# A new order of loads at the pass boundaries, and a new end, in an encoder layer with Strassen-Winograd products

## The chip, the cores and the metric

The kernel runs on one core of one Trainium2 chip. The metric is the device time of one execution in microseconds (us). Timed three times, the kernel before took 2190.53, 2190.92 and 2191.3 us; the median is 2190.92 us.

## The reference

One layer of a streaming encoder, on 2048 prompt rows and 32 rows of a later chunk, with the same weights:

```
h = rms_norm(x, g_mix); p = h @ w_in
mix = concat(pool, conformer conv, short conv, chunk gMLP)(p)
x = x + mix @ w_out
f = rms_norm(x, g_ffn)
x = x + (silu(f @ w_gate) * (f @ w_up)) @ w_down
y = rms_norm(x, g_final)
```

The model width is 1024, the width of w_gate and w_up is 2816. All inputs and outputs are float32. Beside y, the last input rows of the mixers are returned as their new states; the change doesn't touch them.

## The kernel before

**Arithmetic.** Every matrix product is made in three passes of TensorE: an operand is split into a high part (a cast by ScalarE) and a low part (the operand minus its high part), and high x high, low x high and high x low are added up in PSUM. So each weight tile costs a load, a ScalarE cast and a GpSimd subtraction before TensorE can use it, and each row tile costs a cast and a subtraction that GpSimd and VectorE share.

**Stages.** Rows lie as columns (model width on the partitions). The mixer part works in 5 chunks of 416 columns and ends with `w_out_pass(2)`, which finishes `x2[3]` and `x2[4]`. The FFN part works in 6 chunks of 348 or 346 columns, two in each of three passes (`FPASSES`). In a pass the loop over `g` (11 times, `NG`) makes a pair of hidden blocks: `ffn_pair` (L1212) runs `block` once for w_gate (`gate`) and once for w_up (`up`). A block is one Strassen-Winograd product: seven forms named p1, p5, p7, p6, p2, p3, p4 (`ORDER`), each of 12 matmuls (`wide`). After each form stands `then` (L1182), and `step[0]` counts the forms.

**Weights.** `operands` (L1023) loads the four quarters a11, a21, a22, a12 of a block's weights (256 KB each, tag raw, 5 buffers) and makes the seven left operands from them, four of them by additions on VectorE (L1048 to L1059, tile `sum`); `weight_parts` splits each (L1019 on ScalarE, L1020 on GpSimd). `Ahead` makes them `LEAD` = 4 steps before they are used, and loads a block's quarters two at a time.

**Down products.** While a pair is computed, the product of the pair before with w_down is worked off, one `down` (6 matmuls into a `pd` bank of PSUM, then the VectorE addition `xs<-pd,xs` at L1153) after each form or a little oftener, from `LAG` = 3 steps after its pair. 16 of them belong to a pair (8 row tiles m, 2 chunks). Their weights come in four quarters by `quarters` (L1236): two loads of 128 KB (tag rawd, 4 buffers), cast `dhi` (L1253), subtraction `dlo` (L1254).

**Right operands of a pass.** `sums_of` and `first_operands` write the seven row operands to DRAM (`td`). `part` (L953) brings one in, in three steps: the DMA, the cast on ScalarE (L960), the subtraction, half on GpSimd and half on VectorE (L963). They lie in a pool of 5 large tiles (`bigp`), which in the mixers hold `x2[0]` to `x2[4]`. `next_part` (L1431) issues the DMA at one step, and the cast and the subtraction together two steps later.

**Turn of a pass.** When the last pair's down products of a half (m = 3, m = 7) are done, `turn_over` (L1396) writes the two chunks' finished half to DRAM (`away`) and loads the next pass's residual into the same tile (`residual`, `xs<-x2d`). Then `finish` reads the rows back, forms the final norm and writes y.

**The first pair.** Its raw weights go into two tiles that the mixers no longer need (a11, a21, a22, a12 in halves), and a12 and a22 are loaded a second time into `late` tiles (L1056).

**The end.** The last pair's 16 down products run chunk after chunk. For the first chunk of the two, `finish_here` (generator) is worked on between the products of the second, for which squares are made by ScalarE (L1500), added in twos by GpSimd (L1502), and summed over the partitions by small matmuls (L1298) after m = 1, 3, 5, 6 and 7. Then come reciprocal root (L1294), diagonal (L1410), spread over the partitions by a matmul (L1513), scaling of 8 row tiles and the store.

**What sets the order.** Each engine works strictly in the order in which its instructions are issued, the DMA queue of SyncE (SP) too: a DMA that must wait holds all behind it. VectorE and TensorE follow the program text throughout; ScalarE, GpSimd and SP do from the FFN part on. Generators in a list (`ahead`) are advanced by `fill` after each form.

Of the kernel before, what the change touches and what calls it, by code (L numbers as in the profile page):

```python
# [85 lines left out]
def trunk_kernel(ctx: ExitStack, tc: tile.TileContext, a):  # L86
# [936 lines left out]
    def operands(src, g, first=False):  # L1023
# [23 lines left out]
        s3 = wgt.tile([P, H * P], F32, tag="sum", name="sum", bufs=2)  # L1047
        nc.vector.tensor_add(out=s1, in0=a21, in1=a22)  # L1048
        yield weight_parts(a11)
# [5 lines left out]
        if first:  # L1055
            yield None  # L1056
            a12, a22 = (raw_of(*q, raw()) for q in (quads[3], quads[2]))
# [5 lines left out]
    class Ahead:  # L1063
# [15 lines left out]
        def upto(self, step):  # L1079
            while self.made <= step and self.made < 7 * len(self.blocks):  # L1080
                i = self.made // 7
                if not self.made:
                    self.load(0)
                    self.load(0)
                made = next(self.gens[i])
                self.done[self.made] = made if made else next(self.gens[i])
# [17 lines left out]
    for i, _ in enumerate(w_out_pass(2, {  # L1104
        (3, 6): lambda: (start(("fstats", 3), ffn_stats(3)), wq.upto(2)),
        (4, 6): lambda: (whole.add(3), start(("fstats", 4), ffn_stats(4))),
    })):
        if i == 1:
            need(("first", 0))
            for name in ("p7", "p6"):  # L1110
                stage[name] = part(0, name)
                next(stage[name])
    whole.add(4)
# [53 lines left out]
    budget = [1.0]  # L1167

    def block(p, evac, after=lambda k: None):
# [12 lines left out]
        def then():  # L1182
            beside()
            after(step[0] % 7)
            step[0] += 1

# [25 lines left out]
    def ffn_pair(p, g, before, after):  # L1212
# [27 lines left out]
        block(p, up, after)  # L1240
        return hid

    def quarters(g):

        for q in range(H):
            w = []
            for i in range(2):
                raw = late.tile([P, 2 * P], F32, tag="rawd", name="raw", bufs=4)
                nc.sync.dma_start(out=raw, in_=a["w_down"][2 * g + i, :, 2 * q * P : 2 * (q + 1) * P])
# [5 lines left out]
                w.append((hi, lo))  # L1255
            yield w

    def down_later(p, g, hid):
        gen = quarters(g)
# [40 lines left out]
    def full(sq, n):  # L1300

        if n < FN:
            nc.gpsimd.memset(sq[:, n:FN], 1.0)
# [93 lines left out]
    def turn_over(p, h):  # L1397

        for i, c in enumerate(FPASSES[p]):
# [29 lines left out]
    pending = []  # L1429
# [185 lines left out]
```

## Time and profile before

| what | value |
|---|---|
| median of 3 runs | 2190.92 us |
| the profiled execution's own time | 2192.82 us |
| its span, first to last instruction | 2191.1 us |
| mean granted TensorE clock | 0.968 |
| TensorE matmul busy | 2049.9 us (94%) |
| VectorE, ScalarE, GpSimd busy | 1452.4, 760.7, 1128.2 us |

In the views, PE is TensorE, PEld its weight loads, DVE VectorE, ACT ScalarE, POOL GpSimd, SPq the DMA queue of SyncE; L1153 is line 1153 of the kernel. `out<-in` gives the tiles; names in them are the program's. A row of the timeline has start, length, engine, line, operation, and in brackets the idle time before it with what ended that. A row of the windows view has, for a stretch, each engine's busy time with its number of instructions, the granted TensorE clock (1.00 is full speed), the share of DMA time and GB/s. A row of the waits has who waited for whom, total us, times, longest.

### The profile page before, as it was taken

To read this page: it belongs to the slowest core of one execution; us is meant where nothing else is said; L and a number is where in the kernel's file an instruction comes from. 1 tells how busy PE (TensorE), PEld (TensorE's weight loads), DVE (VectorE), ACT (ScalarE), POOL (GpSimd) and SP (SyncE) were. 2 spreads that over 40 slices of the span, in tenths; PEclk is the share of its full clock that TensorE was granted. 3 is DMA by queue.
4 is the path that set the end of the run, shared out by engine and by line. 5 is a ranking of instruction groups with operands and counts; after the bars stand their busy time and mean duration, and the time that the engine had idled before them with its cause. 6 is when DMAs were issued, how large, how long until landed. Compare 5 with 4: busy or idle time off the path is not lost.

```text
span 2191.1 us, 31868 instructions
## 1 busy us (share of the span) xinstructions
PE 2049.9 (94%) x11914; PEld 2003.0 (91%) x11914; DVE 1452.4 (66%) x2198; ACT 760.7 (35%) x1472; POOL 1128.2 (51%) x893
## 2 busy tenths in 40 slices
PE   8799999999996999999998899999998899999995
PEld 7699998898995999999998799999998899999994
DVE  3886598599565677655566577785566577565553
ACT  5433222321423333333333334233333343333331
POOL 2533253243345656566566456566666466665641
PEclk9899999999998999999999999999999999999996
DMA  7634233113476244222243444542243444222211
GB/s 209 176 87 122 63 103 120 48 59 120 168 187 164 90 148 137 74 78 73 73 158 115 136 151 122 162 136 82 78 146 123 136 140 126 87 73 82 78 54 52
DMA packets 152299, 248.41 MB, mean 113 GB/s; under 512 B 23472, under 2 KB 101040, under 8 KB 151504
## 3 DMA queue, kind: packets, MB, share of 16 engines
q1 hardware_dynamic: 149424, 246.19, 36.9%
q8 instruction: 94, 1.54, 0.3%
q10 hardware_dynamic: 2720, 0.18, 0.1%
q14 instruction: 61, 0.50, 0.1%
HBM read 209.95 MB, written 36.36 MB: 112 GB/s over the span
## 4 chain that ended last, share of the span: by engine, by line
PE 54%; DVE 22%; DMA 11%; issue 6%; POOL 3%; ACT 3%; SPq 1%; DVEq 0%; ACTq 0%; POOLq 0%
PE pw L1135 10%; PE pw L1137 10%; PE pw L1136 10%; DVE cv L726 6%; PE pd L1151 6%; PE pd L1152 6%; PE pd L1150 6%; PE ps L230 2%; PE ps L232 2%; PE ps L231 2%; DMA raw<-in_w_down 2%; DMA line<-rt 1%; DVE xs L1153 1%; DMA away<-xs 1%; DMA xk<-in_x 1%
## 5 line engine op out<-in xcount | busy, mean ns | idle before, releaser
L1135 PE MATMUL pw<-f_p,whi 128*128 128x346 f32 (+1 forms) x1848 | 601.0, 325 | 22.8 <-DVE sg L1219 9.7
L1137 PE MATMUL pw<-f_p,whi 128*128 128x346 f32 (+1 forms) x1848 | 599.9, 325 | 3.3 <-POOL f_p L963 3.3
L1136 PE MATMUL pw<-f_p,wlo 128*128 128x346 f32 (+1 forms) x1848 | 598.7, 324 | 0.0
L1020 POOL TENSOR_TENSOR wlo<-sum,whi 128x512 fp32r<-128x512 f32 x264 | 362.7, 1380 | 252.6 <-ACT whi L1019 231.1
L1153 DVE TENSOR_TENSOR xs<-pd,xs 128x346 f32<-128x346 f32 (+1 forms) x528 | 263.6, 512 | 295.5 <-PE pd L1152 295.1
L1135 PEld LDWEIGHTS pw<-f_p,whi 128*128 128x128 f32 x1848 | 354.6, 192 | 25.9 <-issue 18.7
L1150 PE MATMUL pd<-hhi,dhi 128*128 128x346 f32 (+1 forms) x1024 | 332.8, 325 | 37.2 <-ACT dhi L1253 20.5
L1254 POOL TENSOR_TENSOR dlo<-raw,dhi 128x256 fp32r<-128x256 f32 x256 | 209.7, 838 | 300.1 <-ACT dhi L1253 292.8
L1137 PEld LDWEIGHTS pw<-f_p,whi 128*128 128x128 f32 x1848 | 352.5, 191 | 4.4 <-POOL f_p L963 4.4
L1136 PEld LDWEIGHTS pw<-f_p,wlo 128*128 128x128 f32 x1848 | 353.1, 191 | 0.0
L1151 PE MATMUL pd<-hhi,dlo 128*128 128x346 f32 (+1 forms) x1024 | 331.4, 324 | 1.0 <-POOL dlo L1254 1.0
L1152 PE MATMUL pd<-hlo,dhi 128*128 128x346 f32 (+1 forms) x1024 | 330.4, 323 | 0.0
L138 POOL TENSOR_TENSOR wlo<-raw,whi 128x1024 fp32r<-128x1024 f32 x67 | 182.0, 2720 | 272.6 <-ACT whi L137 271.0
L1020 POOL TENSOR_TENSOR wlo<-raw,whi 128x512 fp32r<-128x512 f32 x202 | 288.1, 1432 | 32.6 <-ACT whi L1019 32.6
L230 PE MATMUL ps<-hi,whi 128*128 128x416 f32 x640 | 237.1, 370 | 6.3 <-ACT hi L214 3.0
L231 PE MATMUL ps<-hi,wlo 128*128 128x416 f32 x640 | 230.7, 360 | 5.2 <-POOL wlo L138 5.2
L232 PE MATMUL ps<-lo,whi 128*128 128x416 f32 x640 | 232.4, 363 | 3.1 <-POOL lo L207 2.7
L1019 ACT CAST whi<-sum 128x512 fp32r<-128x512 f32 x264 | 163.1, 618 | 206.8 <-DVE sum L1059 96.8
L1150 PEld LDWEIGHTS pd<-hhi,dhi 128*128 128x128 f32 x1024 | 193.9, 189 | 44.4 <-ACT dhi L1253 21.6
L726 DVE SCALAR_TENSOR_TENSOR cv<-z,par,cv 128x416 f32<-128x416 f32 (+2 forms) x180 | 213.6, 1247 | 0.9 <-ACT cv L720 0.8
L1151 PEld LDWEIGHTS pd<-hhi,dlo 128*128 128x128 f32 x1024 | 193.8, 189 | 2.7 <-POOL dlo L1254 2.3
L1152 PEld LDWEIGHTS pd<-hlo,dhi 128*128 128x128 f32 x1024 | 194.6, 190 | 0.0
(182 smaller groups left out, 2882.5 us busy)
## 6 DMA issues: line engine op xcount, KB each, us to landing
raw<-in_w_gate SPq DMA_DIRECT2D x134, 256.0 KB
raw<-in_w_up SPq DMA_DIRECT2D x132, 256.0 KB
raw<-in_w_down SPq DMA_DIRECT2D x256, 128.0 KB
raw<-in_w_in SPq DMA_DIRECT2D x43, 512.0 KB
raw<-in_w_out SPq DMA_DIRECT2D x24, 512.0 KB
f_p<-td SPq DMA_DIRECT2D x14, 692.0 KB
xt<-in_xt SPq DMA_DIRECT2D x20, 416.0 KB
x<-in_x SPq DMA_DIRECT2D x5, 1664.0 KB
```

The lines of the kernel that those rows point to most:

```text
L230: nc.tensor.matmul(out, whi, xhi, start=start and k == 0, stop=False)
L231: nc.tensor.matmul(out, wlo, xhi, start=False, stop=False)
L232: nc.tensor.matmul(out, whi, xlo, start=False, stop=stop and k == n - 1)
L726: nc.vector.scalar_tensor_tensor(out=cv[:, t, :n], in0=z[:, t, j : j + n], scalar=col("w_conf", 31 * t + j), in1=cv[:, t, :n], op0=ALU.mul ...
L1020: nc.gpsimd.tensor_sub(out=lf, in0=src, in1=hf.bitcast(F32))
L1135: nc.tensor.matmul(ps, whi[:, k], xhi[:, k, :n], start=start and k == 0, stop=False, **more)
L1136: nc.tensor.matmul(ps, wlo[:, k], xhi[:, k, :n], start=False, stop=False, **more)
L1137: nc.tensor.matmul(ps, whi[:, k], xlo[:, k, :n], start=False, stop=stop and k == H - 1, **more)
L1150: nc.tensor.matmul(ps, whi, hhi[:, :n], start=i == 0, stop=False)
L1151: nc.tensor.matmul(ps, wlo, hhi[:, :n], start=False, stop=False)
L1152: nc.tensor.matmul(ps, whi, hlo[:, :n], start=False, stop=i == 1)
L1153: nc.vector.tensor_add(out=xs[c, m], in0=ps, in1=xs[c, m])
```

## The change

**Events.** A list of deferred calls: `at(k, fn)` runs `fn` when `step[0]` has gone k further, at the end of `then`. With it `put_part` replaces `next_part` (DMA, cast two steps later, subtraction one step after that, where the subtraction used to stand with the cast); `turn_over` issues the two `away` writes at once and defers `residual` by 4 steps and `finish` by 8.

**Down weights.** `quarters` now loads ahead: quarters 0 and 1 at step 5 of the up block before (`late_in`), quarter q + 2 right behind the cast and subtraction of quarter q.

**Weight sums.** The sum a21 + a22 is issued after a11's parts and no longer before them: one step later.

**First pair.** All four raw quarters go into one freed `bigp` tile (`raws`), loaded behind the p7 and p6 row operands; nothing is loaded twice, and the parts of a11 are made later (`wq.upto(0)` after (4, 6)). The sums of squares of chunk 3 are finished before the first form instead of after the second.

**The end.** Newly written: no generator and no `finish_here`. Each down product of both chunks is followed by a square on ScalarE, and GpSimd adds them up one by one (6 additions a chunk); the token sums of the first chunk are made after m = 3 of the second, its diagonal after m = 4, its spread after m = 5, its scaling from m = 6 on. `full`'s memset moves from GpSimd to VectorE. The last chunk's scaling reads its scales from SBUF (`rs`), where it read PSUM (`rb`).

```
         if first:
-            pair = [wts.tile([P, D], F32, tag="raw", name="raw", bufs=2) for _ in range(2)]
-            outs = [t[:, i * H * P : (i + 1) * H * P] for t in pair for i in range(2)]
-            a11, a21, a22, a12 = (raw_of(*q, o) for q, o in zip(quads, outs))
+            t = bigp.tile([P, 2 * D], F32, tag="big", name="raws")
+            a11, a21, a22, a12 = (
+                raw_of(*q, t[:, i * H * P : (i + 1) * H * P]) for i, q in enumerate(quads)
+            )
...
+        yield weight_parts(a11)
         nc.vector.tensor_add(out=s1, in0=a21, in1=a22)
-        yield weight_parts(a11)
         nc.vector.tensor_sub(out=s3, in0=a11, in1=a21)
...
-            a12, a22 = (raw_of(*q, raw()) for q in (quads[3], quads[2]))
...
+    def at(k, fn):
+        events.append((step[0] + k, fn))
+        events.sort(key=lambda e: e[0])
...
             step[0] += 1
+            while events and events[0][0] <= step[0]:
+                events.pop(0)[1]()
...
+        def late_in(k):
+            if k == 5 and gen:
+                next(gen)
+            after(k)
...
+        def load(q):
+            if q < H:
+                raws[q] = [late.tile([P, 2 * P], F32, tag="rawd", name="raw", bufs=4) for _ in range(2)]
+                for i, raw in enumerate(raws[q]):
+                    nc.sync.dma_start(out=raw, in_=a["w_down"][2 * g + i, :, 2 * q * P : 2 * (q + 1) * P])
+        load(0)
+        load(1)
+        yield
         for q in range(H):
...
+            load(q + 2)
             yield w
...
             nc.sync.dma_start(out=away[c, h][:, : H * n], in_=halfs[c, h][:, : H * n])
-            residual(FPASSES[p + 1][i], h)
+            at(4, lambda i=i: residual(FPASSES[p + 1][i], h))
         if h:
-            for c in FPASSES[p]:
-                start(("finish", c), finish(c))
+            at(8, lambda: [start(("finish", c), finish(c)) for c in FPASSES[p]])
...
+    def put_part(p, name, first=1):
+        gen = part(p, name)
+        for k in (first, first + 2):
+            at(k, lambda: next(gen))
+        at(first + 3, lambda: [None for _ in gen])
...
+    def squared(i, m):
+        c = FPASSES[last][i]
+        sq = rowf("sq")
+        full(sq, n)
+        nc.scalar.activation(out=sq[:, :n], in_=xs[c, m], func=AF.Square)
+        if m % 7:
+            nc.gpsimd.tensor_add(out=sq[:, :n], in0=sq[:, :n], in1=acc[i, 0][:, :n])
+        acc[i, m // 7] = sq
...
     for m in range(KT):
         last_down(1, m)
+        squared(1, m)
+        if m == 3:
+            rt = total(0)
+        if m == 4:
+            dg = spread_diagonal(rt)
+        if m == 5:
+            rs = spread_scales(dg)
+        if m >= 6:
+            for k in (2 * m - 12, 2 * m - 11):
+                scaled(ca, k, rs)
+    dg = spread_diagonal(total(1))
+    for k in range(4, KT):
+        scaled(ca, k, rs)
+    for h in range(2):
+        out_rows(ca, h)
+    rs = spread_scales(dg)
+    for h in range(2):
+        by_pool(cb, h * H + 3, rs)
+        for k in range(3):
+            scaled(cb, h * H + k, rs)
+        out_rows(cb, h)
```

**What it moves.** First, the SP queue at the first pass boundary, from the last weights ahead of the first `away` write on. Before:

```order
L1402 DMA away<-xs 128x1392
L1424 DMA xs<-x2d 128x4x346
L1402 DMA away<-xs 128x1392
L1424 DMA xs<-x2d 128x4x346
L1249 DMA raw<-in_w_down 128x256 x2
L1027 DMA raw<-in_w_up 128x512 x2
```

After:

```order
L1425 DMA away<-xs 128x1392 x2
L1265 DMA raw<-in_w_down 128x256 x4
L1446 DMA xs<-x2d 128x4x346 x2
L1027 DMA raw<-in_w_up 128x512 x2
L1265 DMA raw<-in_w_down 128x256 x2
```

The first quarter of down weights behind the writes no longer stands behind the residual loads that must wait for those writes. Second, the SP queue at the start of the FFN part (`f_p` are the row operands, first p7 and p6, then p2, later p3 and p4; `rline` is the write of the FFN norm's scales). Before:

```order
L958 DMA f_p_4853<-td 128x1392
L339 DMA x2d<-x_4352 128x6x416
L1027 DMA raw<-in_w_gate 128x512 x2
L339 DMA x2d<-x_4416 128x6x416
L339 DMA x2d<-x_4352 128x2x416
L1027 DMA raw<-in_w_up 128x512 x2
L1027 DMA raw<-in_w_gate 128x512 x2
L958 DMA f_p_5206<-td 128x1392
```

After:

```order
L958 DMA f_p_4853<-td 128x1392
L1027 DMA raws<-in_w_gate 128x512 x4
L339 DMA x2d<-x_4352 128x6x416
L339 DMA x2d<-x_4416 128x6x416
L339 DMA x2d<-x_4352 128x2x416
L1027 DMA raw<-in_w_up 128x512 x2
L339 DMA x2d<-x_4416 128x2x416
L958 DMA f_p_5208<-td 128x1392
```

The first block's weights go ahead of the copies of `x2`, and the second load of two quarters is gone. Third, VectorE in the last up block of the first pass, from the first row operand's subtraction on (`u` and `sg` take the banks of a block's fourth form). Before:

```order
L963 TENSOR_TENSOR f_p_10241<-f_p_10241 128x692
L1048 TENSOR_TENSOR sum<-raw 128x512
L1197 TENSOR_TENSOR u_10325<-pw,r_10231 128x348
L1199 TENSOR_TENSOR u_10327<-pw,u_10325 128x348
L1227 TENSOR_TENSOR u_10327<-pw,u_10327 128x348
L1229 TENSOR_TENSOR sg<-u_10327,sg 128x348
```

After:

```order
L1205 TENSOR_TENSOR u_10321<-pw,r_10230 128x348
L1207 TENSOR_TENSOR u_10323<-pw,u_10321 128x348
L1235 TENSOR_TENSOR u_10323<-pw,u_10323 128x348
L1237 TENSOR_TENSOR sg<-u_10323,sg 128x348
L1241 TENSOR_TENSOR hlo<-sg,hhi 128x348
L1152 TENSOR_TENSOR xs<-pd,xs 128x348 x2
L963 TENSOR_TENSOR f_p_10240<-f_p_10240 128x692
L1050 TENSOR_TENSOR sum<-raw 128x512
```

The block's banks are now taken before the subtraction and before the sum that waits for raw weights.

More of the change, by code (lines that the diff above doesn't have):

```diff
@@ L1081, in upto @@
                 i = self.made // 7
[L1082 to L1086, printed above, removed]
+                self.done[self.made] = next(self.gens[i])
                 self.made += 1
@@ L1112, in trunk_kernel @@
                 next(stage[name])
+            while ("squares", 2) not in made:
+                next(made["fstats", 2])
+            wq.load(0)
+            wq.load(0)
     whole.add(4)
@@ L1459, in first_parts @@
                     residual(c, h)
+    while ("squares", 3) not in made:
+        next(made["fstats", 3])
     active[0] = 1
@@ L1489, in last_down, with total @@
         )
+    acc = {}
+    def squared(i, m):
[6 more added lines that the diff above has]
+        acc[i, m // 7] = sq
+    def total(i):
+        tok = ps_ax.tile([P, 512], F32, tag="ax", name="tok")[:FTB, :FNB]
+        for j in range(FNB):
+            for h in range(2):
+                sums(tok[:, j : j + 1], acc[i, h], j, h == 0, h == 1)
+        return token_scales([tok])
@@ new lines, in spread_scales, with by_pool @@
+    def spread_scales(dg):
+        r = ps_ax.tile([P, 512], F32, tag="ax", name="rb")
+        nc.tensor.matmul(r[:, :FN], ones[:FTB], dg[:FTB, :FN], start=True, stop=True)
+        rs = rowf("rs")
+        nc.scalar.copy(out=rs[:, :n], in_=r[:, :n])
+        return rs
+    def by_pool(c, k, rs):
+        x = xs[c, k]
+        g = rowf("g")
+        nc.scalar.activation(out=g[:, :n], in_=x, func=AF.Copy, scale=col("g_final", k))
+        nc.gpsimd.tensor_mul(out=x, in0=g[:, :n], in1=rs[:, :n])
@@ L1491, in trunk_kernel @@
+    while ahead:
+        fill(100.0)
     for m in range(KT):
         last_down(0, m)
-    ahead.append(finish_here(ca))
-    toks = [ps_mm.tile([P, 512], F32, tag="mm", name="tok")[:FTB, :1] for _ in range(FNB)]
-    prev_sq = None
+        squared(0, m)
     for m in range(KT):
         last_down(1, m)
-        sq = rowf("sq")
-        full(sq, n)
-        nc.scalar.activation(out=sq[:, :n], in_=xs[cb, m], func=AF.Square)
-        if m in (1, 3, 5):
-            nc.gpsimd.tensor_add(out=sq, in0=sq, in1=prev_sq)
-        prev_sq = sq
-        fill(1.2)
-        if m in (1, 3, 5, 6, 7):
-            for j in range(FNB):
-                sums(toks[j], sq, j, m == 1, m == 7)
@@ L1508, in trunk_kernel @@
-    rt = token_scales(toks)
-    for _ in iter(lambda: fill(100.0) or bool(ahead), False):
-        pass
-    dg = spread_diagonal(rt)
-    r = ps_ax.tile([P, 512], F32, tag="ax", name="rb")
-    nc.tensor.matmul(r[:, :FN], ones[:FTB], dg[:FTB, :FN], start=True, stop=True)
-    rs = rowf("rs")
-    nc.scalar.copy(out=rs[:, :n], in_=r[:, :n])
-    for k in range(KT):
-        if k % H == H - 1:
-            x = xs[cb, k]
-            g = rowf("g")
-            nc.scalar.activation(out=g[:, :n], in_=x, func=AF.Copy, scale=col("g_final", k))
-            nc.gpsimd.tensor_mul(out=x, in0=g[:, :n], in1=rs[:, :n])
-            out_rows(cb, k // H)
-        else:
-            scaled(cb, k, r)
+        squared(1, m)
```

57 lines of the change are left out of this document (21 added, 36 removed).

## The prediction

> **What bounds the kernel now.** I read the page, then the windows view over the FFN part, then the waits of TensorE in the stretches that come out short, then the timelines of the engines that it waited for there. The page, and one steady stretch of 50 us:
>
> ```profile
> span 2191.1 us, 31868 instructions
> PE 2049.9 (94%) x11914; PEld 2003.0 (91%) x11914; DVE 1452.4 (66%) x2198; ACT 760.7 (35%) x1472; POOL 1128.2 (51%) x893
> ...
> 900.00:950.00 50.00, 50.00 (x316) 50.00 (x315) 28.16 (x51) 18.15 (x39) 29.45 (x26) 1.00 0.25 75
> ```
>
> TensorE is the bound: in the steady stretch it does 316 matmuls in 50 us, 0.158 us each, with no idle time at full clock, and the change leaves that number of matmuls nearly as it is. So only stretches can be won where fewer come out. They are these: the start of the FFN part, one mid-pass stretch for each of passes 0 and 1, the two pass boundaries (three rows each), and the end:
>
> ```profile
> 660.00:727.00 67.00, 45.91 (x240) 43.77 (x240) 39.25 (x52) 24.64 (x45) 34.22 (x24) 0.82 0.57 143
> 810.00:870.00 60.00, 55.65 (x345) 54.47 (x344) 46.54 (x75) 21.49 (x47) 36.02 (x30) 1.00 0.50 150
> 1130.00:1180.00 50.00, 44.92 (x259) 43.81 (x258) 37.13 (x49) 21.62 (x38) 38.31 (x29) 0.93 0.41 140
> 1180.00:1235.00 55.00, 44.43 (x256) 43.25 (x255) 25.20 (x42) 13.67 (x31) 20.61 (x18) 0.91 0.55 174
> 1235.00:1262.00 27.00, 24.38 (x153) 23.46 (x152) 20.05 (x33) 12.15 (x27) 17.77 (x16) 1.00 0.23 68
> 1380.00:1450.00 70.00, 65.94 (x408) 64.08 (x407) 58.70 (x92) 23.33 (x52) 40.27 (x35) 1.00 0.52 155
> 1640.00:1680.00 40.00, 34.89 (x206) 33.79 (x205) 28.60 (x38) 19.02 (x33) 34.01 (x25) 0.96 0.34 114
> 1680.00:1735.00 55.00, 44.05 (x254) 42.84 (x253) 24.86 (x42) 15.05 (x34) 20.64 (x21) 0.91 0.53 167
> 1735.00:1765.00 30.00, 27.59 (x170) 26.46 (x169) 24.49 (x41) 11.36 (x25) 20.15 (x16) 1.00 0.31 95
> 2132.00:2192.00 60.00, 34.44 (x162) 30.35 (x160) 24.11 (x50) 11.41 (x25) 11.62 (x20) 0.69 0.12 48
> ```
>
> Length minus 0.158 us times the matmuls (first bracket) is what a stretch loses: start 67 - 38.0 = 29.0; mid-pass 5.4 and 5.5; boundary 1: 9.0 + 14.5 + 2.8 = 26.3; boundary 2: 7.4 + 14.8 + 3.1 = 25.3. The end has 59 us for 162 matmuls. Busy time doesn't show this (44.43 of 55), because waits also lower the granted clock (0.91), and matmuls at a lower clock count as busy.
>
> **Boundaries.** The waits of TensorE in 1180 to 1235, then ScalarE's and SP's rows behind them:
>
> ```profile
> PE pd L1150 <- ACT dhi L1253: 10.0, 2, 7.7
> ...
> 1194.04 0.77 ACT L1253 CAST dhi<-raw 128x256 fp32r<-128x256 f32 x2 [8.65 <-DMA raw<-in_w_down]
> 1225.04 0.76 ACT L1253 CAST dhi<-raw 128x256 fp32r<-128x256 f32 x2 [14.49 <-DMA raw<-in_w_down]
> ...
> 1211.08 0.46 SPq L1402 DMA_DIRECT2D away<-xs  x1
> 1219.39 0.37 SPq L1424 DMA_DIRECT2D xs<-x2d  x1
> 1220.83 0.90 SPq L1249 DMA_DIRECT2D raw<-in_w_down  x2
> ```
>
> SP stands from 1211.1 to 1219.4, because the residual may only be loaded over a half that has been written away; the down weights stand behind it, ScalarE waits 14.49 us for them (8.65 at the other half's turn), and TensorE 10.0 us for ScalarE. In the new order the first two quarters are loaded before their pair is done, the others one quarter ahead, and the residual follows its write by 4 steps; a step is a form and a down product, 18 matmuls or 2.85 us, so 4 steps are 11.4 us, longer than the 8.3 us that the write held SP. The residual is next read by the new pass's first down products: for either half some 4 steps after its load is issued, which hides it. Of the 14.5 and 14.8 us I take 13.5 each back: 27. What is late next there is VectorE. In 1130 to 1180 it is busy 37 of 50 us, with these two rows for the same subtraction, alone and beside a GpSimd row:
>
> ```profile
> 1142.34 0.88 DVE L963 TENSOR_TENSOR f_p<-f_p 128x692 fp32r<-128x692 f32 x1 [0.27 <-ACT f_p L960]
> 1147.02 2.38 DVE L963 TENSOR_TENSOR f_p<-f_p 128x692 fp32r<-128x692 f32 x1
> ...
> 1146.98 1.69 POOL L963 TENSOR_TENSOR f_p<-f_p 128x692 fp32r<-128x692 f32 x1 [0.68 <-ACT f_p L960]
> ```
>
> The change removes VectorE's wait for the cast (the subtraction comes one step later, behind one more weight split on GpSimd; its operand is used 7 steps after its load and is ready after 4, so this costs nothing) and puts the evacuation of the banks ahead of the weight sum; it removes no work. I take 2 us of the 9.0 and 2 of the 7.4. The third rows (2.8, 3.1) belong to the final norm that starts there; it now starts 8 steps later, with its squares, additions and row loads on SP, in a stretch with less else to do: 1 each. Boundaries together: 27 + 4 + 2 = **33 us**; bounds 20 (half of the first term comes back as something else) and 46 (all but 5.6 of 51.6).
>
> **Mid-pass stretches** lose 5.4 and 5.5 us at clock 1.00. The sum a21 + a22, over the whole program:
>
> ```profile
> L1048 DVE TENSOR_TENSOR sum<-raw 128x512 f32<-128x512 f32 x66 | 83.3, 1263 | 23.3 <-DMA raw<-in_w_gate 19.8 <-DMA raw<-in_w_up 3.0 <-DMA td<-t 0.5
> ```
>
> Its mean is 1.26 us, and its 3.5 us of waits for in_w_up and td fall mid-pass, each ahead of a bank evacuation. It now stands behind the evacuation, one step later; ScalarE's cast of it comes later too, but 4 steps ahead of use. I take **4 us**; bounds 0 and 9.
>
> **Start.** TensorE's waits from 660 to 727, then SP, ScalarE and VectorE:
>
> ```profile
> PE pw L1135 <- ACT f_p L960: 7.0, 1, 7.0
> PE tok L147 <- DVE ssum L346: 6.2, 2, 4.7
> PE pw L1135 <- DVE u L1227: 4.6, 1, 4.6
> ...
> 676.33 0.90 SPq L958 DMA_DIRECT2D f_p<-td  x2
> ...
> 689.40 1.35 ACT L960 CAST f_p<-f_p 128x1392 fp32r<-128x1392 f32 x1 [3.64 <-DMA f_p<-td]
> ...
> 654.98 0.69 DVE L1048 TENSOR_TENSOR sum<-raw 128x512 f32<-128x512 f32 x1 [9.83 <-DMA raw<-in_w_gate]
> 710.86 0.69 DVE L1048 TENSOR_TENSOR sum<-raw 128x512 f32<-128x512 f32 x1 [10.01 <-DMA raw<-in_w_gate]
> ```
>
> VectorE stood 9.83 us for the first block's raw weights while the additions that complete x2[3], x2[4] and the sums of squares were queued behind; the 6.2 us of token sums follow from that. The new loads are ahead of the copies of x2, and the sum stands behind four of those additions: this wait goes. The 10.01 us went to the second block's evacuation (4.6 us of TensorE); it now stands ahead of the sum. What stays: p3 and p4. Their loads left at 676.33 and were cast at 689.40. They stand on SP behind the scales' write, which waits for GpSimd; that chain starts some 8 us earlier (an estimate: the 9.83 us, less what is queued before it). But p4's tile is now that of `raws`: its load waits until GpSimd has split the last raw quarter, and queued behind it on SP are the second scales' write and the next raw weights. TensorE, without the 6.2 us and the low clock behind them, comes to p3 earlier by more than those 8 us, and waits longer than 7.0 us for it. So of 29.0 I take **13 us**; bounds 5 (p4's new wait uses up the rest) and 22 (only p3's 7.0 stays).
>
> **End.** The rows on which it rests:
>
> ```profile
> PE tok L1298 <- POOL sq L1303: 10.0, 3, 4.7
> PE rb L1513 <- DVE dg L1410: 5.2, 1, 5.2
> ...
> 2173.85 1.32 PE L1298 MATMUL tok<-ones,sq 128*116 128x1 f32 x6 [1.14 <-ACT sq L1500]
> ...
> 2134.45 5.03 POOL L1020 TENSOR_TENSOR wlo<-raw,whi 128x512 fp32r<-128x512 f32 x4 [7.14 <-ACT whi L1019]
> ...
> L1502 POOL TENSOR_TENSOR sq<-sq 128x348 f32<-128x348 f32 x3 | 2.7, 916 | 23.8 <-ACT sq L1500 23.8
> L1521 POOL TENSOR_TENSOR xs<-g,rs 128x346 f32<-128x346 f32 x2 | 1.8, 918 | 8.0 <-ACT g L1520 8.0
> ```
>
> From 2132 on 20 down products of 6 matmuls remain, 120 x 0.158 = 19.0 us; the last token sums began at 2173.85, so 23 us there are waits and low clock. In the new end two things stand in TensorE's way: the first chunk's token sums (1.3 us) and the matmul that spreads its scales (about 1), and a wait for the diagonal, since VectorE's diagonal waits for GpSimd's root and the additions that free the `pd` banks are queued behind it: an estimate of 2 us, under the 5.2 that the same wait took, and 1.2 for lower clock behind it. So the last sums begin at 2132 + 19 + 5.5 = 2156.5, 17.3 us earlier. The squares' 12 additions cost GpSimd 12 x 0.916 = 11.0 us, begin behind the splits that end at 2139.5, and have until about 2156: no bound. From the last sums to the end it took 17.2 us, and the new tail has the same steps. **17 us**; bounds 13 (GpSimd's chain, or VectorE's, comes last) and 23.
>
> In the rows above one subtraction of VectorE took 0.88 us alone and 2.38 beside GpSimd's. The Trainium skill ("SBUF — State Buffer", section "Who interferes with whom") says that a VectorE instruction with two SBUF inputs excludes a GpSimd instruction that reads SBUF, the later one blocking altogether, and one with a single SBUF input doesn't. By that rule, which speaks against this end, the last scaling, whose scales now lie in SBUF, would alternate with GpSimd's two multiplications: up to their 1.8 us more, and the end would give 15 us; the sum stays with 17.
>
> **The sum.** 33 + 4 + 13 + 17 = 67 us. The profiled execution took 2192.82 us, 1.7 more than its span and 1.9 more than the median of the runs, 2190.92. 2192.82 - 67 = 2125.8, and 2190.92 - 67 = **2124 us** as a median.
>
> **Rivals.**
> - *The next late thing takes the place* (0.18): VectorE's and GpSimd's work at the boundaries is not reduced, and the p3 and p4 loads still bound the start. For it: 37 of 50 us busy and the 2.38 us row. Against: TensorE's own longest waits name ScalarE and the down weights. With 20 + 0 + 5 + 13 = 38 us: 2153.
> - *More goes* (0.08): 46 + 9 + 22 + 23 = 100 us: 2091.
> - *Slower by the new wait on SP* (0.04). The load of quarter q + 2 needs the tile of quarter q, whose subtraction has only just been issued; SP stands until GpSimd is through, with the next block's raw weights behind it. It happens twice in each of 32 pairs. Waits of GpSimd and ScalarE in the steady 900 to 1100 us:
>
> ```profile
> POOL dlo L1254 <- ACT dhi L1253: 37.1, 10, 4.0
> ...
> L1254 POOL TENSOR_TENSOR dlo<-raw,dhi 128x256 fp32r<-128x256 f32 x256 | 209.7, 838 | 300.1 <-ACT dhi L1253 292.8
> ```
>
> GpSimd was held at most 4.0 us for that cast; with 2 x 0.84 us for the two subtractions SP stands at most 6 us. The raw quarters behind it are issued some two steps (5.7 us) later, so nearly all of it lies in time that SP has. It decides from 67 / 32 = 2.1 us of TensorE per pair on; at 3 us it would be 2124 + 96 = 2220. A steady pair would then take 43 us and not 40.
> - *The end alone fails* (0.1): if squares, roots and banks wait for each other, it gives 8: 2133.
>
> **Chances and range.** Forecast as summed 0.6. The unknown costs' bounds lie 10 to 15 us about it in most combinations; to hold 8 in 10 the range takes in the failing end, part of the first rival and of the second: **2100 to 2150**. Over 0.2% (4.4 us, about what a measurement of this kernel can tell from no change) faster: all but the slower rival and 0.01 of the first, 0.95; within: 0.02; slower: 0.03, most of the slower rival.
>
> **What would show it.** In the profile after: no row of ScalarE's `dhi` waiting over 3 us for in_w_down at a boundary; 1180 to 1235's successor with 340 matmuls or so in 55 us; TensorE waiting at the start for p3 or p4 only; the last token sums about 17 us before the old place relative to the last forms; steady stretches still 316 in 50 us. Wrong it would be if steady stretches lose matmuls, if a boundary still loses over 15 us, or if TensorE waits over 5 us in one place of the end.

## The result and the profile after

The changed kernel took 2126.57 us (median of 4 runs, 2122.69 to 2128.51), the kernel before 2190.73 in the same series. The ratio is 0.971, with a 95% interval of 0.9689 to 0.9731: 3% faster. The forecast was 2124, range 2100 to 2150. So the time came out as predicted, but two of the four terms behind it did not: the boundaries gave 27 us where 33 were forecast, the end 21 where 17 were. That the sum fits so closely is luck: the errors of the terms (-5.7 at the boundaries, +4.2 at the end, +1.6 in the middle of the passes) cancel.

The profiled execution of the changed kernel took 2125.5 us, 67.3 less than that of before. The page, and the windows that answer to those shown of before:

```profile
span 2123.8 us, 31916 instructions
PE 2027.5 (95%) x11902; PEld 1980.8 (93%) x11902; DVE 1444.6 (68%) x2207; ACT 767.5 (36%) x1472; POOL 1138.5 (54%) x891
```

```profile
660.00:715.00 55.00, 43.97 (x244) 41.47 (x243) 30.78 (x42) 22.15 (x40) 35.60 (x26) 0.84 0.59 158
900.00:950.00 50.00, 50.00 (x316) 50.00 (x315) 26.12 (x47) 17.21 (x35) 29.20 (x25) 1.00 0.24 75
1120.00:1160.00 40.00, 34.92 (x207) 32.49 (x206) 33.73 (x42) 19.15 (x33) 33.73 (x23) 1.00 0.38 130
1160.00:1215.00 55.00, 55.00 (x348) 55.00 (x347) 31.03 (x54) 20.37 (x45) 34.63 (x32) 1.00 0.54 183
1215.00:1245.00 30.00, 27.26 (x169) 26.43 (x168) 23.69 (x36) 12.93 (x30) 16.15 (x14) 1.00 0.37 113
1280.00:1330.00 50.00, 46.62 (x284) 45.79 (x283) 37.86 (x62) 20.95 (x46) 29.74 (x26) 0.97 0.34 108
1640.00:1695.00 55.00, 55.00 (x348) 55.00 (x347) 31.53 (x57) 20.50 (x45) 34.94 (x31) 1.00 0.54 184
2085.00:2123.00 38.00, 25.68 (x155) 23.43 (x154) 22.33 (x59) 12.20 (x25) 20.55 (x20) 0.86 0.19 75
```

The middle row of each boundary, where the kernel before did 256 and 254 matmuls in 55 us, is now a steady stretch: 348 in 55 us at full clock. But the rows around it did not empty: 1215 to 1245 loses 30 - 0.158 x 169 = 3.3 us, more than the 2.8 of before, and 1280 to 1330 loses 5.1.

Windows cut both kernels at different work. A sharper measure is the same instruction in both: VectorE's evacuations of `pw` stand in the same sequence, 363 of them, so that the n-th of before and the n-th of after mark the same point of the program. Five of them, first of before, then of after (start, length, engine, line, operation):

```profile
789.85 0.51 DVE L1197 TENSOR_TENSOR u<-pw,r 128x348 f32<-128x348 f32 x1
...
1120.11 0.52 DVE L1219 TENSOR_TENSOR sg<-pw,u 128x348 f32<-128x348 f32 x1 [0.79 <-PE pw L1137]
...
1374.28 0.52 DVE L1199 TENSOR_TENSOR u<-pw,u 128x346 f32<-128x346 f32 x1
...
1569.18 0.52 DVE L1219 TENSOR_TENSOR sg<-pw,u 128x346 f32<-128x346 f32 x1
...
2060.50 0.52 DVE L1199 TENSOR_TENSOR u<-pw,u 128x346 f32<-128x346 f32 x1
```

```profile
776.66 0.51 DVE L1205 TENSOR_TENSOR u<-pw,r 128x348 f32<-128x348 f32 x1
...
1105.97 0.52 DVE L1227 TENSOR_TENSOR sg<-pw,u 128x348 f32<-128x348 f32 x1 [0.80 <-PE pw L1136]
...
1346.67 0.52 DVE L1207 TENSOR_TENSOR u<-pw,u 128x346 f32<-128x346 f32 x1
...
1536.86 0.52 DVE L1227 TENSOR_TENSOR sg<-pw,u 128x346 f32<-128x346 f32 x1
...
2014.37 0.52 DVE L1207 TENSOR_TENSOR u<-pw,u 128x346 f32<-128x346 f32 x1
```

The differences are 13.19, 14.14, 27.61, 32.32 and 46.13 us, and 67.3 at the span's end. Between two such points lies what a stretch gave:

| stretch | forecast | gained |
|---|---|---|
| start | 13 | 13.2 |
| mid-pass of pass 0 | 2 | 0.9 |
| boundary 1 | 16.5 | 13.5 |
| mid-pass of pass 1 | 2 | 4.7 |
| boundary 2 | 16.5 | 13.8 |
| end | 17 | 21.2 |
| sum | 67 | 67.3 |

The experiments below are measured in the same way against the changed kernel ("gained" or "lost" in a stretch). How much such a figure scatters is seen where a kernel was not altered: the kernel with the old end, the same up to the end, differs there by 0.1 to 0.3 us in four stretches and by 2.6 in one, and the kernel with the norm 14 steps later, not altered at the start, differs there by 3.7. So differences below 3 us in one stretch (below 4 at the start) say little. The runs were made on several chips, on which the kernel before took 2187.1 to 2190.9 us as a median; times of different runs compare to within about 4 us, ratios better.

### The profile page after: what moved, and what is told of

Same layout as the page of the kernel before. It is cut to its first block, busy times and chain, and to the rows that moved or that the text cites. A ratio compares the mean times of both kernels' runs of the same rounds, so it can differ in the third digit from the quotient of the medians.

```text
span 2123.8 us, 31916 instructions
## 1 busy us (share of the span) xinstructions
PE 2027.5 (95%) x11902; PEld 1980.8 (93%) x11902; DVE 1444.6 (68%) x2207; ACT 767.5 (36%) x1472; POOL 1138.5 (54%) x891
## 4 chain that ended last, share of the span: by engine, by line
PE 51%; DVE 18%; issue 11%; POOL 10%; DMA 7%; ACT 2%; SPq 1%; POOLq 0%; DVEq 0%; ACTq 0%
PE pw L1136 8%; PE pw L1134 8%; PE pw L1135 8%; DVE cv L726 6%; POOL wlo L1020 6%; PE pd L1150 5%; PE pd L1149 5%; PE pd L1151 5%; PE ps L230 4%; PE ps L232 4%; PE ps L231 3%; POOL dlo L1277 2%; DMA line<-rt 2%; DMA xk<-in_x 1%; POOL f_p L963 1%
## 5 line engine op out<-in xcount | busy, mean ns | idle before, releaser
L1136 PE MATMUL pw<-f_p,whi 128*128 128x346 f32 (+1 forms) x1848 | 598.4, 324 | 10.6 <-POOL f_p L963 10.5
L1020 POOL TENSOR_TENSOR wlo<-sum,whi 128x512 fp32r<-128x512 f32 x264 | 354.6, 1348 | 288.7 <-ACT whi L1019 285.7
L1136 PEld LDWEIGHTS pw<-f_p,whi 128*128 128x128 f32 x1848 | 350.1, 189 | 13.6 <-POOL f_p L963 13.6
L1277 POOL TENSOR_TENSOR dlo<-raw,dhi 128x256 fp32r<-128x256 f32 x256 | 223.0, 891 | 227.3 <-ACT dhi L1276 224.6
L1020 POOL TENSOR_TENSOR wlo<-raw,whi 128x512 fp32r<-128x512 f32 x199 | 275.4, 1392 | 36.6 <-ACT whi L1019 36.4
```

What stands on the lines that cost most here:

```text
L1020: nc.gpsimd.tensor_sub(out=lf, in0=src, in1=hf.bitcast(F32))
L1136: nc.tensor.matmul(ps, whi[:, k], xlo[:, k, :n], start=False, stop=stop and k == H - 1, **more)
L1277: nc.gpsimd.tensor_sub(out=lf, in0=raw, in1=hf.bitcast(F32))
```

## The experiments

All start from the changed kernel. The first three ask which of two edits took the down weights' wait away.

**Residual at once.**

```
-            at(4, lambda i=i: residual(FPASSES[p + 1][i], h))
+            residual(FPASSES[p + 1][i], h)
```

> The changed kernel with one part undone: the residual load follows its write at once again (no 4 steps between), while the first two quarters of the down weights are still loaded early. From the changed kernel's 2126.6 us. Theory A (the deferral of the residual carries the gain of the boundaries): at each boundary SP stands some 8 us again, and most of the 28 us of both boundaries is lost, at least 16: 2143 or more, with ScalarE waiting over 5 us for in_w_down there. Theory B (the early load of the down weights carries it): at most 6 us are lost, 2127 to 2133, and the two residual loads hold only loads that have time. Theory C (either is enough, since each alone takes the down weights out of the queue behind the held residual): the same 2127 to 2133 here; it is told from B by the next run. By SP's rows I expect the first quarters to leave at about 1176 and not 1171.8, 3.5 us ahead of the cast that needs them: 0 to 2 us a boundary.

2128.77 us (ratio to the kernel before 0.9718, 0.9694 to 0.9743). Both boundaries together neither gained nor lost (+1.8 and -1.7). Its SP queue at the first turn:

```profile
1165.10 0.38 SPq L1425 DMA_DIRECT2D away<-xs  x1
1169.32 0.38 SPq L1446 DMA_DIRECT2D xs<-x2d  x1
1169.79 0.46 SPq L1425 DMA_DIRECT2D away<-xs  x1
1176.44 0.37 SPq L1446 DMA_DIRECT2D xs<-x2d  x1
1176.87 1.93 SPq L1265 DMA_DIRECT2D raw<-in_w_down  x4
```

SP stands for each residual as it did before, and the four loads behind leave from 1176.9 on, where they left from 1165.8 on in the changed kernel. But they are loads for a pair whose products are still to come: ScalarE waited 0.5 us for them at this boundary and 1.5 at the other. A held queue costs only what somebody needs by then. Theory A is out.

**Down weights loaded where they are cast.**

```
-        load(0)
-        load(1)
         yield
         for q in range(H):
             w = []
-            for raw in raws.pop(q):
+            for i in range(2):
+                raw = late.tile([P, 2 * P], F32, tag="rawd", name="raw", bufs=4)
+                nc.sync.dma_start(out=raw, in_=a["w_down"][2 * g + i, :, 2 * q * P : 2 * (q + 1) * P])
...
-            load(q + 2)
             yield w
```

> The changed kernel with the other part undone: each quarter of the down weights is loaded where it is cast, as before, while the residual stays 4 steps behind its write. Theory A (the deferral carries the gain): at most 6 us are lost, 2127 to 2133. Theory B (the early load carries it): 16 us or more are lost, 2143 and up, with ScalarE waiting over 5 us for in_w_down at the boundaries. Theory C (either is enough): 2127 to 2133 here and in the run before.

2127.48 us (0.971, 0.9693 to 0.9727). The boundaries lost 0.2 us together: theory B is out too, and C stands. What this run lost lies elsewhere: 3.3 us in the mid-pass of pass 0 and 4.1 in that of pass 1.

**Both undone.** The two edits above together.

> The changed kernel with both undone: residual at once, quarters loaded where they are cast. All of A, B and C expect what the boundaries gained to be lost, but for the change of VectorE's order and the later finish: 27 us by the prediction's sum, so 2153; ScalarE waits 8 and 14 us for in_w_down at a boundary as in the kernel before. A rival D, that the boundaries gained by the three-step row operands and by VectorE's order and not by the down weights, expects no more than 10 us: 2137.

2164.77 us (0.9878, 0.9856 to 0.99): 38 us of the 64 are gone, 14.3 and 17.0 of them at the two boundaries and 7.2 in the mid-passes. That is more than the 27 us expected. ScalarE's rows of the casts, at the two turns of the first boundary, and TensorE's waits from 1160 to 1240:

```profile
1182.39 0.79 ACT L1268 CAST dhi<-raw 128x256 fp32r<-128x256 f32 x2 [10.71 <-DMA raw<-in_w_down]
...
1212.22 0.79 ACT L1268 CAST dhi<-raw 128x256 fp32r<-128x256 f32 x2 [13.56 <-DMA raw<-in_w_down]
```

```profile
PE pd L1149 <- ACT dhi L1268: 11.2, 2, 6.7
```

These are the rows of before again (8.65, 14.49 and 10.0). So the wait was what the prediction said it was, and either edit alone removes it: one lets the residual leave the queue, the other lets the weights overtake it. D is out.

**Norm at once.**

```
-            at(8, lambda: [start(("finish", c), finish(c)) for c in FPASSES[p]])
+            for c in FPASSES[p]:
+                start(("finish", c), finish(c))
```

> The changed kernel with the final norm of a finished pass started at once, not 8 steps later. The prediction gave the deferral 1 us a boundary: 2 us are lost, 2128 to 2129. Rival: the third rows of both traces lose the same (2.8 before, 3.2 after), so the deferral gives nothing: 2126 to 2127 and TensorE's waits for xs additions only move some 22 us earlier. A second rival: the rows that finish reads stand on SP ahead of the down weights again and hold them, 6 us or more: 2133 and up.

2113.03 us (0.9644, 0.963 to 0.9658): 13.5 us faster than the changed kernel. All three expectations missed; the deferral, for which the prediction had put 2 us on the gain side, costs 12.8 at the boundaries (7.6 and 5.2). TensorE's waits behind the first boundary, 1195 to 1335 in the changed kernel, then 1185 to 1330 in this one:

```profile
PE pd L1149 <- DVE xs L1152: 5.0, 3, 2.4
PE pw L1134 <- DVE sg L1227: 1.1, 2, 1.0
```

```profile
PE pd L1149 <- DVE xs L1152: 0.4, 1, 0.4
PE pw L1134 <- DVE sg L1227: 0.2, 1, 0.2
```

VectorE holds TensorE up by the additions that free `pd` banks. Its rows in the changed kernel show what stands ahead of them, the additions of the norm's squares (L1349):

```profile
1229.19 1.35 DVE L1057 TENSOR_TENSOR sum<-raw,sum 128x512 f32<-128x512 f32 x1
1231.62 1.30 DVE L1349 TENSOR_TENSOR ssum<-ssum,sq 128x348 f32<-128x348 f32 x1 [1.08 <-ACT sq L1347]
1232.85 0.50 DVE L1152 TENSOR_TENSOR xs<-pd,xs 128x346 f32<-128x346 f32 x1
1233.28 1.16 DVE L1349 TENSOR_TENSOR ssum<-ssum,sq 128x348 f32<-128x348 f32 x1
1234.36 0.50 DVE L1152 TENSOR_TENSOR xs<-pd,xs 128x346 f32<-128x346 f32 x1
```

A gate block evacuates its banks with five VectorE instructions, an up block with thirteen (the product with the gate and the low part besides). Of the 14 additions behind boundary 1, 8 run ahead of a block's first evacuation in the changed kernel, in this one and in the kernel before. The other 6 run among the evacuations of a gate block with the norm at once and in the kernel before, and among those of an up block in the changed kernel. Eight steps are one block and one step: they move the norm into the denser block. That the norm's place costs the 12.8 us is shown; that it does so by the denser block is a reading, and not all of it: in the kernel before, with the 6 among a gate block's evacuations, TensorE still waited 3.5 us for `xs` behind that boundary (1230 to 1370).

**Norm 14 steps later.** `at(14, ...)` for `at(8, ...)`.

> The changed kernel with the final norm started 14 steps after the last turn, not 8. Started at once, the kernel took 13.5 us less. Theory P (phase): the 8 steps move VectorE's seven additions of squares from a gate block, where an evacuation takes 1 or 3 instructions, into an up block, where it takes 3 to 5 with the hlo; 14 steps are a whole pair, so the additions fall into a gate block again, and most of the 13.5 us comes back: 2113 to 2119. Theory E (early): the norm has to be done while the turn still has VectorE idle, each step later costs; 14 is as bad as 8 or worse: 2126 to 2132. Theory Q (queue): the reads of the rows hold SP ahead of the down weights (12.7 us in the changed kernel, 7.4 and 9.4 with the norm at once); with 14 steps ScalarE's or TensorE's waits for loads decide, and either time is possible.

2127.94 us (0.9731, 0.9709 to 0.9754): taken as a whole, as bad as 8 steps. By stretch it splits. Behind boundary 2 it gained 6.1 us, as the norm at once did (5.2), with 1 of the 14 additions among an up block's evacuations; TensorE's waits there, 1640 to 1850, in the changed kernel and in this one:

```profile
PE pd L1149 <- DVE xs L1152: 5.0, 3, 2.4
PE pw L1134 <- DVE sg L1227: 1.0, 2, 0.8
```

```profile
PE pd L1149 <- DVE xs L1152: 0.5, 1, 0.5
PE pw L1134 <- DVE sg L1227: 0.2, 1, 0.2
```

So the theory of the phase fits where nothing else comes in, and "the later the worse" is out there. Behind boundary 1 it lost 2.8 and in the mid-pass 3.9: 14 steps later the row operands of the next pass (`sums_of`, from g = 2) are already in the list ahead of the norm, and the norm runs some 105 us later than in the changed kernel. Pass 2 has no such work. That this order is the cause of those 6.7 us was not tried by itself.

**Weight sum first.**

```
-        yield weight_parts(a11)
         nc.vector.tensor_add(out=s1, in0=a21, in1=a22)
+        yield weight_parts(a11)
```

> The changed kernel with the weight sum a21 + a22 issued ahead of a11's parts again, one step earlier. From the changed kernel's 2126.6 us. The prediction's theory: the sum, which waits for raw weights, stands ahead of a bank's evacuation on VectorE; undone, the mid-pass stretches lose 4 us, the boundaries up to 4, and the start the 4.6 us of the second block: 8 to 13 us, 2135 to 2140. Rival: the run with late down weights already lost 1 to 2 us at the mid-pass of pass 0 and 4 us in pass 1, about all that the mid-pass stretches had gained, so that it is the early down loads that take the sum's raw weights out of a crowded queue; then the sum's place is worth 0 to 5 us, at the start alone: 2127 to 2132.

2127.99 us (0.9734, 0.9713 to 0.9754), as its rival said. The start lost 4.9, and the row that the prediction named for 4.6 us is back, VectorE's sum ahead of the second block's banks:

```profile
701.40 0.69 DVE L1049 TENSOR_TENSOR sum<-raw 128x512 f32<-128x512 f32 x1 [7.02 <-DMA raw<-in_w_gate]
702.01 0.51 DVE L1205 TENSOR_TENSOR u<-pw,r 128x348 f32<-128x348 f32 x1
```

The mid-passes lost 0.9 and 3.0, but boundary 1 gained 5.1 and boundary 2 0.8: there the sum's new place is, if anything, the worse one.

**Row operands as before.** `put_part` loads at `first`, casts and subtracts at `first + 2`, with `first = 0`.

> The changed kernel with the row operands of the next pass brought in as before: the load right behind the form (not a step later), cast and subtraction together two steps behind the load; the same for p2, p3 and p4 at the start. Theory of the prediction: VectorE's wait for the cast comes back ahead of the banks, about 2 us at each boundary's first row: 2130 to 2131. Rival: the three-step form made new waits of its own (TensorE 3.0 us a boundary for GpSimd's f_p, because GpSimd has one more split ahead of it), so that undoing it gains up to 3 us a boundary: 2121 to 2126.

2125.88 us (0.9723, 0.9701 to 0.9744): no difference that stands out. Boundaries +2.0 and -3.2, about the scatter. What TensorE waits for in the first row changes, from 2.5 us for VectorE's `xs` and 2.5 for GpSimd's `f_p` to 4.7 for VectorE's `xs`; how long it waits doesn't. Both engines are busy 33.7 of 40 us there, and the steps' order only says which of them is last.

**Neither, norm at once.** The edits of "both undone" and of "norm at once" together.

> The changed kernel with the residual at once, the down weights loaded where they are cast, and the final norm started at once: the boundaries' loads and norm as in the kernel before. The norm started at once gained 13.8 us at the boundaries of the changed kernel; with the down weights held, the norm 8 steps later cost only about 4 more than the kernel before lost. Theory H (cover): while TensorE stands for the down weights, VectorE works off the norm for nothing, so that its start hardly matters there: 4 us less than the run with neither (2164.8), 2159 to 2162, and both boundaries lose what they lost in the kernel before, 27 to 29 us more than in the changed kernel. Theory S (sum): the two costs add up independently: 13.8 us less, 2151, and some 10 us of the boundaries' gain have another cause that no run has found.

2161.19 us (0.9869, 0.9852 to 0.9885): the time of theory H, but not by its reason. Both boundaries together, against the changed kernel:

| | norm at once | norm 8 steps later |
|---|---|---|
| down weights late, residual at once | -32.0 | -31.3 |
| down weights early, residual later | +12.8 | 0 |

With the down weights late, the norm's place makes no difference (0.7 us); once that wait is gone, the place is worth 12.8 us. The two costs do not add up independently, so theory S is out. But theory H's cover is not what the trace shows. TensorE, ScalarE and VectorE at the second turn of the first boundary:

```profile
1214.30 0.65 PE L1149 MATMUL pd<-hhi,dhi 128*128 128x346 f32 x1 [7.90 <-ACT dhi L1268]
...
1215.42 0.48 ACT L1338 ACTIVATE sq<-xf 128x348 f32<-128x348 f32 x1
...
1215.93 1.42 DVE L1340 TENSOR_TENSOR ssum<-ssum,sq 128x348 f32<-128x348 f32 x1 [15.30 <-ACT sq L1338]
```

TensorE went on at 1214.30. The norm's first addition began 1.6 us later, and VectorE had stood 15.30 us for its square, which stands on ScalarE behind the cast that waits for the down weights. So no addition of the norm was made while TensorE stood; the kernel before shows the same (TensorE went on at 1225.50, the first addition began at 1227.13). TensorE's waits at that boundary show two sides instead. For `dhi` it waited 12.4 us, and 11.2 with the norm 8 steps later; at the second turn two loads of the norm's rows now stand on SP ahead of the down weights. For `xs` it waited 3.3 us behind the turn, 5.6 with the norm later, but 0.4 in the kernel with the norm at once and the weights early. So with the weights late, starting the norm at once lengthens one wait and shortens the other by less than elsewhere. How much of the 12.8 us each of the two takes was not tried by itself.

The kernel before lost 27.3 us in the count of the table; the 4.7 us between it and the kernel of this run belong to what else differs there (the operands' steps, the sum's place, the scatter), and no run settles them.

**The old end.** The end of the kernel before, with `full` on GpSimd.

> The changed kernel with the end of the kernel before. By the traces the new end gave 21.3 us: 17.6 up to the last token sums, 3.6 behind them, where the second chunk's diagonal stood 4.7 us behind the first chunk's eight scalings: 2148, with all of the loss behind the last form and 17.2 us from the last token sums to the end. Rival: part of the 21.3 us is due to what comes ahead (GpSimd and SP arrive at the end with less queued, since the loads are earlier): the old end loses only the 17 us of the prediction or less: 2143 or under.

2147.81 us (0.9823, 0.98 to 0.9846): 21.2 us slower by the medians, as the trace of before had it, and some 25 by the ratios. The profiled execution, 3.2 us above that median, lost 23.3 behind the last form, 2.6 behind boundary 2 and nothing elsewhere. The rival is out.

**Three edits to go on.** The norm at once, the last scaling from PSUM, `put_part(p + 1, ORDER[k], 0)`:

```
-            scaled(cb, h * H + k, rs)
+            scaled(cb, h * H + k, r)
```

> The changed kernel with three edits: the final norm of a pass started at once (2113.0 us by itself), the last scaling of the second chunk reading its scales from PSUM as in the kernel before, and the row operands of the next pass loaded, cast and subtracted one step earlier. The three touch separate places, so the trace shows each. On the last scaling: theory, VectorE with scales in SBUF shuts out GpSimd's two multiplications (six took 4.35 us beside 2.47 of GpSimd, against 3.00 and 1.79 before): from PSUM they take 3.0 and 1.8 again and the end is 1.3 us shorter. Rival: the six are slower for another reason (the place of the tiles), and nothing changes. On the row operands: theory, the waits for GpSimd's f_p (3.0 us a boundary) go, up to 6 us in all. Rival, for which the run with the old row operands speaks (it gave nothing): VectorE's and GpSimd's work in that stretch is the bound, and another wait takes the place: 0. Sum: 2106 to 2112 by the theories, 2111 to 2112 if only the scaling gains.

2108.46 us (0.9637, 0.9618 to 0.9656). VectorE's last scaling and GpSimd's two multiplications, in the changed kernel:

```profile
2115.39 4.35 DVE L1330 SCALAR_TENSOR_TENSOR xs<-xs,par,rs 128x346 f32<-128x346 f32 x6 [0.20 <-ACT rs L1528]
```

```profile
2115.91 2.47 POOL L1535 TENSOR_TENSOR xs<-g,rs 128x346 f32<-128x346 f32 x2 [3.24 <-ACT g L1534]
```

and with the scales read from PSUM:

```profile
2100.47 3.00 DVE L1330 SCALAR_TENSOR_TENSOR xs<-xs,par,rb 128x346 f32<-128x346 f32 x6 [0.20 <-ACT rs L1529]
```

```profile
2101.00 1.79 POOL L1536 TENSOR_TENSOR xs<-g,rs 128x346 f32<-128x346 f32 x2 [3.23 <-ACT g L1535]
```

1.35 us less on VectorE and 0.68 on GpSimd, as the theory had it. By the rule of the Trainium skill ("SBUF — State Buffer", section "Who interferes with whom"), that a VectorE instruction with two inputs in SBUF and a GpSimd instruction that reads SBUF exclude each other, this is to be expected, and the traces agree: the same instructions with one input in PSUM run side by side at 0.50 and 0.90 us each. The end gained 0.8 us of the 1.35 in this trace. The row operands gave 0.1 and 1.8 us more than the norm alone: nothing that stands out of the scatter.

**Row operands' subtraction on VectorE alone.** Norm at once and scales from PSUM, and in `part` both halves by `nc.vector`.

> The changed kernel with the norm started at once and the last scales from PSUM, and the subtraction of every row operand whole on VectorE (two halves one after the other), none of it on GpSimd. The two halves at once took 1.9 us on VectorE and 2.0 to 2.3 on GpSimd in the boundary's first row, 0.86 on VectorE when alone. Theory S (the two engines shut each other out, so that the split buys nothing): whole on VectorE it takes 1.7 us, less than the half did, GpSimd has 2 us less to do per operand, and the 6 us that the first row of each boundary loses shrink: 4 to 10 us in all, 2102 to 2108. Rival V: VectorE is the bound there, its own additions for the banks wait behind 0.86 us more for each operand: no gain or 5 us more, 2111 to 2117.

2115.44 us (0.9666, 0.9648 to 0.9684), 2.4 slower than the norm alone, and 7.0 slower than the three edits on the same chip: rival V, boundaries 2.4 and 4.1 us behind the norm alone. The two halves took 1.7 us at best, but 2.2 to 3.4 in most places of the boundaries, beside GpSimd's splits of weights. So the split in halves does share the work, though both sides of it slow down.

**Order in the end.** The three edits, and the spread after m = 6, four scalings after m = 7:

```
-        if m == 5:
+        if m == 6:
...
-        if m >= 6:
-            for k in (2 * m - 12, 2 * m - 11):
+        if m == 7:
+            for k in range(4):
```

> The kernel of three edits (2108.5 us) with two places of the end moved: the spread of the first chunk's scales one product later (after m = 6), and all four early scalings of the first chunk behind the last addition of a down product (after m = 7), none between m = 6 and m = 7. In the changed kernel TensorE stood 0.64 us for that diagonal and 1.4 us longer for a bank, because VectorE had two scalings (0.98 us) ahead of the addition that frees it. Theory: the last token sums begin 1.5 to 2 us earlier after the last form, the time is 2106.5 to 2107. Rival: the four scalings now stand ahead of VectorE's step for the mean square and push the root and the last diagonal back by as much: 2108 to 2109.

2105.89 us (0.962, 0.9605 to 0.9635), the lowest ratio here and below both expectations; its interval overlaps that of the three edits, so the two are not told apart, and lies below that of the changed kernel. By the trace the last token sums come 0.9 us earlier behind the last form, half of what was expected, and TensorE's wait for the last diagonal behind them grows from 1.75 to 2.12 us.

## Why the prediction was right, and where it was wrong

**Bound.** Right: steady stretches still do 316 matmuls in 50 us, and all of the gain lies in the stretches named.

**Boundaries, 33 forecast, 27.3 measured.** The mechanism, down weights behind a held residual on SP, is shown by the run with both edits undone; no ScalarE row waits for in_w_down there any more. What failed is the rest of the term.
- *27 for the down weights* was too small. With the norm's place as in the changed kernel the wait is worth 31.3 us, with the norm at once 44.8 (12.8 + 32.0). The prediction priced the wait by what the middle row lost and put the norm down as a term of its own, but the two depend on each other.
- *4 for VectorE's order*: the operands' steps gave nothing, the sum's place cost 1 to 5 us at a boundary. The prediction's own remark, "it removes no work", was the right one. With both engines at 33.7 of 40 us, order shifts the wait from one to the other.
- *2 for the later norm* had the wrong sign: it costs 12.8. The step that failed was "in a stretch with less else to do". Only the stretch's mean was read, not which instructions of VectorE the additions would stand among. With the norm at once the boundaries gain 40.1 us, near the 46 of the rival "more goes".

**Mid-pass, 4 forecast, 5.6 measured.** About right, by a cause that was half seen. The sum's place is worth 0.9 and 3.0 us, the early down loads 3.3 and 4.1. In pass 1, where 4.7 us were gained, undoing either gives back most of it, so both seem to be needed; in pass 0 the 0.9 gained is within the scatter.

**Start, 13 forecast, 13.2 measured.** The size is right, the parts less so. TensorE's waits from 658 to 715:

```profile
PE pw L1136 <- POOL f_p L963: 5.5, 2, 3.2
PE pw L1134 <- ACT f_p L960: 3.0, 1, 3.0
PE tok L147 <- DVE ssum L346: 2.5, 1, 2.5
```

The wait for VectorE before the second block (4.6) is gone, by the sum's place as said. The token sums still cost 2.5 of 6.2. The wait for p3's cast went down from 7.0 to 3.0 where the prediction had it grow: the load left 8 us earlier (676.33 to 668.10), as estimated, and its cast 10.6 us earlier. The waits for GpSimd's subtraction grew from 3.3 to 5.5: 2.3 for p2 and 3.2 for p3, whose third matmul needs the low part. So p3 cost 6.1 us in all, and 8.5 before; TensorE waits some 0.3 us for p4, whose new place in the queue the prediction feared. Of the 13.2 us, 1.9 were already there at the first form (660.40 to 658.51); other executions of the same mixers came there up to 4 us apart, so that this part may be scatter. The old load order was not tried by itself.

**End, 17 forecast, 21.2 measured.** Up to the last token sums it went as worked out: from the last form's products to them 41.8 us before and 24.2 now, 17.6 gained for 17.3 forecast. The four more lie behind: "the new tail has the same steps" was wrong. TensorE's row that waits for the diagonal, in the kernel with the old end:

```profile
2139.06 1.50 PE L1527 MATMUL rb<-dg,ones 116*128 116x348 f32 x2 [5.16 <-DVE dg L1432]
```

In the old end VectorE scales all eight tiles of the first chunk ahead of the second's diagonal; in the new text the diagonal comes first and four scalings behind it, while TensorE and ScalarE work. In the changed kernel that wait is 1.75 us. It shows in the two ends' code, and the prediction read the steps without their order. From the last token sums to the end it is 17.2 us before and 13.6 now.

**Slower by SP.** Rightly given little, though with too small a figure. SP's waits from 860 to 1100:

```profile
SPq L1265 <- POOL dlo L1277: 147.3, 34, 9.0
```

It stands up to 9.0 us, not at most 6, and for 147 of 240 us; yet the same point of each pair stays 14.14 us early throughout that time, so that it cost nothing. All of SP's waits there come to 194 us, in the kernel before too, where SP waited mostly for VectorE's sums instead. What counts is not how long the queue stands but whether the loads behind it have that much time left. (A steady pair is 264 matmuls, so 41.8 us and not the 40 that the prediction gave.)

## What to carry to other kernels

What a wait is worth depends on what else is changed with it: removing this one gave 31.3 us with the norm late and 44.8 with the norm at once, and the norm's place began to matter only when the wait was gone. Before giving a reason for that, look in the trace when the other work ran; the idea that it was done under cover of the wait is a natural one, and here the rows say otherwise. When work is deferred, look at which instructions it will stand among and not only at how busy the stretch is on average: eight steps more, for a stretch with less to do, cost 12.8 us. And where two edits aim at one wait, undo each alone and both together; here either was enough, and undoing one alone would not have shown what the wait was worth.

## What the runs showed of the hardware

The granted clock fell behind waits that were not long, but not each time. Windows of the changed kernel, three behind boundary 1 and one behind boundary 2:

```profile
1220.00:1240.00 20.00, 17.26 (x106) 16.43 (x105) 15.69 (x25) 8.79 (x20) 10.18 (x9) 1.00 0.25 79
...
1300.00:1320.00 20.00, 17.58 (x110) 17.02 (x109) 15.95 (x27) 6.97 (x16) 6.87 (x8) 1.00 0.20 60
1320.00:1340.00 20.00, 20.00 (x119) 19.79 (x118) 11.20 (x21) 8.35 (x18) 15.20 (x13) 0.91 0.35 110
...
1800.00:1820.00 20.00, 20.00 (x127) 19.79 (x128) 11.53 (x22) 9.21 (x20) 16.08 (x15) 1.00 0.37 114
```

In the first, with two waits of at most 1.7 us, the clock stayed at 1.00. Near the end of the second TensorE stood once for 2.40 us, and in the third it did 119 matmuls instead of the 126 or so that fit, with hardly an idle moment, at 0.91: that wait cost its 2.4 us and about 1.1 more. But at the same place behind boundary 2 TensorE stood 2.39 us, up to 1799.8, and did 127 matmuls at 1.00 in the last window. In the run with the residual at once, behind the same wait of 2.40 us at boundary 1, TensorE did 127 matmuls from 1320 to 1340 at 1.00. So the length of a wait alone did not decide here, and this is a part of the scatter between executions.
